# A two-layer fp32 encoder: mask by VectorE, an earlier-placed index selection, and an order of instructions from the tile framework's timeline simulator

## The chip, the cores and the metric

The kernel runs on one core of a Trainium2 chip. The metric is the device time of one execution in microseconds. The kernel before takes 315.13 us (median of three runs, 314.31 to 315.16).

## The reference

x has 256 tokens of 1024 features, fp32. Two layers follow one another, each with a gate and a post-norm. Layer 0 is attention over selected keys, layer 1 is stick-breaking attention, both with 16 heads of 64.

```python
# layer 0 (dsa_mixer): an indexer of 8 heads scores all keys, the best 64 admissible ones stay
q, k, v, g, qi, wi, ki = split(x @ w_in)          # q, k, qi, ki get rope
score = einsum('bqhs,bqh->bqs', relu(qi @ ki.T * 64 ** -0.5), wi)
idx = top_k(where(adm, score, -inf), 64)          # adm: key chunk <= query chunk, chunks of 64
o = softmax(where(selected, q @ k.T * 64 ** -0.5, -inf)) @ v
y = (o * silu(g)) @ w_out
# layer 1 (stick_breaking_mixer)
z = q @ k.T * 64 ** -0.5
log_one_minus = where(before, log_sigmoid(-z), 0)           # before: key position < query position
log_stick = cumsum(log_one_minus, reverse) - log_one_minus
y = ((where(before, exp(log_sigmoid(z) + log_stick), 0) @ v) * silu(g)) @ w_out
# after each layer
x = layer_norm(ALPHA * x + y, ln_g[i], ln_b[i])
```

## The kernel before

Every fp32 operand of a matmul is kept as a high part (rounded to the fp32r type by a ScalarE copy) and a low part (VectorE subtracts); `split` (L65) and `feat_split` (L247) do that, and a product is three matmuls: high by high, low by high, high by low. In the trace `wh`/`wl`, `xT`, `yT`, `zh`/`zl`, `oh`/`ol` are such pairs.

Weights come in 80 chunks of 128x1024 fp32 (512 KB) from `w_all`, by `fetch` (L79), through 4 raw buffers and 8 buffers each of `wh` and `wl`; a copy `wh` can start when its chunk has landed and the matmuls that read the buffer's former chunk are done. A chunk feeds 12 matmuls of 512 columns where an output block of 512 columns is computed for the two row blocks t = 0, 1 of 128 tokens (`tok_block`, L116), or one gate (`proj_feat`, L140: 24 matmuls of 256 columns).

Layer 0: the index projection runs over the 8 chunks of `x_idx` (L221 to L230), rope follows on VectorE (`rope`, L211), then `select` (L280) runs beside the q, k and v projections of the first half of the heads: score matmuls (L136 to L138 by `mm3`), Relu on ScalarE, weighting on VectorE, and eight rounds of max and match_replace per row block (L299, L300), which end in the masks `nm0` and `nm1` (L304). The head pairs pass through four stages in a loop of 11 steps (L525): `keys0`, `logits0` (min-reduce on VectorE L420, Exp on ScalarE L425, scaling of p by VectorE L430), `turn0` (transposes of p, L439 to L441, copy `pT` L443), `values0`. A generator `fill` puts the other projections, the eight gates and the out-projection between them. The out-projection with its norm is `out_norm` (L454): residual `z` (L461), statistics (L463, L467), power on GpSimd (L470), two passes over z and x (L473, L475); `turn` (L514) transposes x into `yT` for layer 1. The second row block's right half is computed in two banks of 256 columns.

Layer 1: v, the gates (`proj_feat1`, L148), then head pairs in five stages (L619); `logits1` (L564) adds the causal mask with an identity matmul (L576) and goes through Abs, Exp, Ln on ScalarE and a combination on VectorE (L582); `sticks1` sums along keys by matmuls with a triangle. Then `out_norm` again with stores.

Each engine works through its instructions in one fixed order. That order isn't the program's: the tile framework's scheduler sets it at build time from the dependences, except where `keep_in_program_order` pins an instruction. PSUM is shared by a pool `pp` of three banks and `at` of five.

## Time and profile before

| | |
|---|---|
| median of three runs | 315.13 us |
| profiled execution | 313.89 us, its span 312.1 us |
| TensorE busy | 299.8 us (96%), 1722 matmuls |
| VectorE busy | 246.3 us (79%) |
| ScalarE busy | 191.7 us (61%) |
| GpSimd busy | 7.7 us |
| DMA | 50.40 MB, mean 161 GB/s |

The span is that of one profiled execution; the run's time holds some 1.8 us around it. Busy shares are means over stages. The rows further down have times in us from the span's start.

### The profile page before, as it was taken

The numbers are of one execution on the slowest core, as the hardware profiler recorded it, in microseconds if no ns is written. First come the engines' busy times: TensorE is split into PE (matmuls) and PEld (weight loads), VectorE is DVE, ScalarE is ACT, GpSimd is POOL, SyncE is SP. The second block draws the span as 40 slices with busy tenths as digits, with TensorE's granted clock in tenths as the row PEclk, the third lists the DMA queues.
The fourth block names the chain that finished last, engine by engine and source line by source line (L and its number), as shares of the span: only waits on it lengthen the run. The fifth ranks groups of instructions, "written<-read, shape, count | busy, mean of one in ns | idle before, by whom it ended". The sixth has DMA issues, their size and how long they took to land.

```text
span 312.1 us, 4825 instructions
## 1 busy us (share of the span) xinstructions
PE 299.8 (96%) x1722; PEld 256.3 (82%) x1722; DVE 246.3 (79%) x538; ACT 191.7 (61%) x388; POOL 7.7 (2%) x16
## 2 busy tenths in 40 slices
PE   8998799998999999999999999999999999999990
PEld 5986688886888899988888888888888888887790
DVE  3777989998999999997589576776788887872375
ACT  5655445385346998875415377657799998975200
POOL 3010000000000000000010100000000000000011
PEclk9999799999999999999999999999999999999997
DMA  7898736586044846574424858866553253000003
GB/s 255 270 328 284 274 111 202 186 280 209 4 131 137 268 138 187 186 234 140 133 67 127 275 161 295 287 197 198 167 163 100 69 159 100 2 0 2 0 13 121
DMA packets 14423, 50.40 MB, mean 161 GB/s; under 512 B 1600, under 2 KB 1728, under 8 KB 14400
## 3 DMA queue, kind: packets, MB, share of 16 engines
q1 hardware_dynamic: 14256, 49.97, 49.3%
q8 instruction: 13, 0.21, 0.3%
q10 hardware_dynamic: 144, 0.14, 0.1%
q14 instruction: 10, 0.08, 0.1%
HBM read 49.05 MB, written 1.05 MB: 161 GB/s over the span
## 4 chain that ended last, share of the span: by engine, by line
PE 78%; DVE 10%; DMA 6%; issue 3%; ACT 2%; DVEq 0%; SPq 0%; ACTq 0%
PE bank L113 32%; PE bank L153 14%; PE bank L145 7%; PE bank L155 7%; DMA raw<-w_all 4%; DVE wl L67 4%; PE bank L368 3%; DMA raw<-x_idx 2%; PE bank L596 1%; PE bank L136 1%; PE bank L369 1%; DVE sc L293 1%; ACT wh L66 1%; DVE sc L300 1%; PE bank L138 1%
## 5 line engine op out<-in xcount | busy, mean ns | idle before, releaser
L67 DVE TENSOR_TENSOR wl<-raw,wh 128x1024 fp32r<-128x1024 f32 (+2 forms) x89 | 103.5, 1165 | 23.1 <-ACT wh L66 22.4
L66 ACT ACTIVATE wh<-raw 128x1024 fp32r<-128x1024 f32 (+2 forms) x89 | 90.0, 1016 | 50.2 <-DMA raw<-w_all 25.6
L113 PE MATMUL bank<-wh,xT 128*128 128x512 f32 x192 | 50.8, 400 | 1.2 <-DVE rb L216 1.2
L153 PE MATMUL bank<-yT,wh 128*128 128x512 f32 x192 | 48.3, 394 | 0.0
L113 PEld LDWEIGHTS bank<-wh,xT 128*128 128x128 f32 x192 | 35.9, 191 | 8.7 <-issue 1.6
L153 PEld LDWEIGHTS bank<-yT,wh 128*128 128x128 f32 x192 | 34.5, 189 | 6.9 <-issue 0.3
L155 PEld LDWEIGHTS bank<-yT,wl 128*128 128x128 f32 x192 | 26.2, 190 | 1.9
L113 PE MATMUL bank<-wl,xT 128*128 128x512 f32 x96 | 27.6, 396 | 0.0
L155 PE MATMUL bank<-yT,wl 128*128 128x256 f32 x192 | 26.8, 282 | 0.0
L113 PEld LDWEIGHTS bank<-wl,xT 128*128 128x128 f32 x96 | 18.4, 192 | 3.7
L113 PE MATMUL bank<-wh,ol 128*128 128x512 f32 (+1 forms) x80 | 20.5, 350 | 0.0
L113 PE MATMUL bank<-wh,oh 128*128 128x512 f32 (+1 forms) x80 | 20.4, 354 | 0.0
L113 PE MATMUL bank<-wl,oh 128*128 128x512 f32 (+1 forms) x80 | 20.2, 348 | 0.0
L113 PE MATMUL bank<-wh,yT 128*128 128x512 f32 x64 | 17.4, 391 | 0.0
L145 PE MATMUL bank<-xT,wh 128*128 128x256 f32 x128 | 16.9, 285 | 0.0
L425 ACT ACTIVATE p<-ml,mx 128x128 f32<-128x128 f32 (+1 forms) x32 | 14.3, 447 | 3.7 <-DVE mx L420 3.4
L145 PEld LDWEIGHTS bank<-xT,wh 128*128 128x128 f32 x128 | 16.1, 190 | 0.4
L113 PEld LDWEIGHTS bank<-wh,ol 128*128 128x128 f32 x80 | 14.1, 189 | 2.1 <-issue 0.2
L113 PEld LDWEIGHTS bank<-wl,oh 128*128 128x128 f32 x80 | 14.1, 189 | 1.9
L113 PEld LDWEIGHTS bank<-wh,oh 128*128 128x128 f32 x80 | 13.6, 189 | 2.2 <-issue 0.5
L113 PEld LDWEIGHTS bank<-wh,yT 128*128 128x128 f32 x64 | 12.0, 188 | 2.4
L582 DVE SCALAR_TENSOR_TENSOR ab<-bank,ab 128x512 f32<-128x512 f32 (+1 forms) x16 | 8.5, 555 | 6.3 <-ACT ab L581 5.9
(140 smaller groups left out, 507.3 us busy)
## 6 DMA issues: line engine op xcount, KB each, us to landing
raw<-w_all SPq DMA_DIRECT2D x80, 512.0 KB, 4.3
raw<-x_idx SPq DMA_DIRECT2D x7, 420.0 KB, 4.1
gb<-lnp SPq DMA_DIRECT2D x4, 512.0 KB, 6.9
x<-x_rows SPq DMA_DIRECT2D x2, 512.0 KB, 6.5
y<-x SPq DMA_DIRECT2D x4, 256.0 KB, 2.0
cs<-consts SPq DMA_DIRECT2D x1, 512.0 KB, 6.8
raw<-x_idx SPq DMA_DIRECT2D x1, 288.0 KB, 2.9
raw<-x_idx ACTq DMA_DIRECT2D x1, 132.0 KB, 3.1
```

What stands on the lines that cost most here:

```text
L66: nc.scalar.activation(h, src, AF.Copy)
L67: nc.vector.tensor_sub(lo, src, as32(h))
L113: nc.tensor.matmul(ps, src[kk][xp][:, t * P:(t + 1) * P], wc[wp][:, k, :], start=kk == 0 and xp + wp == 0, stop=kk == 7 and wp == 1)
L136: nc.tensor.matmul(ps, sh, mh, start=first, stop=False)
L138: nc.tensor.matmul(ps, sl, mh, start=False, stop=last)
L145: nc.tensor.matmul(ps, w[wp][:, k, :], src[k][xp], start=k + xp + wp == 0, stop=k == 7 and wp == 1)
L153: nc.tensor.matmul(ps, wh[:, k, :], yT[:, k], start=k == 0, stop=k == 7)
L155: nc.tensor.matmul(ps[:, :S], wl[:, k, :], yTh[:, k], start=False, stop=k == 7, skip_group_check=True)
L293: nc.vector.scalar_tensor_tensor(sc, rel[:, a, :], wi[t][:, h:h + 1], prev, op0=OP.mult, op1=OP.add)
L368: nc.tensor.matmul(po[rs, n * S:(n + 1) * S], vt[0][:, hs], p0(i), start=True, stop=False)
L425: nc.scalar.activation(p[:, i, :], m[:, i, :], AF.Exp, bias=mx[:, c], scale=-1.0, accum_out=sm[:, c])
L582: nc.vector.scalar_tensor_tensor(a, pv, 0.0, a, op0=OP.max, op1=OP.add)
```

## The change

What the source does differently, in the order of the program:

1. `load` pins the loads on SyncE's queue to the program's order. Before, layer 0's gains and biases (`gb`) and x's rows stood at places 17 to 23 of that queue, among the loads for the q and k blocks; now they stand at places 35 to 44, one after each step of the loop from step 4 on.
2. The first chunk of `x_idx` comes in three DMAs instead of two, chunks 1 and 3 are issued from ScalarE's queue, and VectorE copies the first `xT`.
3. `rope` adds both halves with one instruction, whose second operand has its halves swapped.
4. The transposes of the index queries and keys move into `select` and start two steps later; the scores of both row blocks are computed alternately, and both top-k follow.
5. p is scaled by ScalarE (a Copy with a scale per row) instead of VectorE.
6. The causal mask of layer 1 is added in PSUM by VectorE (16 adds of 128x256) instead of by 16 matmuls.
7. Layer 1's gains and biases are loaded inside its gate loop.
8. `schedule_with_timeline_sim=True`: the order of instructions on every engine comes from the framework's timeline simulator.

```diff
+    def load(dst, src):
+
+        tc.keep_in_program_order(nc.sync.dma_start(dst, src))
...
-        nc.sync.dma_start(raw, w_all[c])
+        load(raw, w_all[c])
...
         if k:
-            nc.sync.dma_start(raw, x_idx[k])
+            (nc.scalar.dma_start if k in (1, 3) else load)(raw, x_idx[k])
         else:
             first = S + IDX_A
-            nc.sync.dma_start(raw[:, :first], x_idx[k, :, :first])
-            nc.scalar.dma_start(raw[:, first:], x_idx[k, :, first:])
+            load(raw[:, :S], x_idx[k, :, :S])
+            nc.scalar.dma_start(raw[:, S:first], x_idx[k, :, S:first])
+            load(raw[:, first:], x_idx[k, :, first:])
...
+        if k:
+            split(xTh[:, k], xTl[:, k], raw[:, :S])
+        else:
+            nc.vector.tensor_copy(xTh[:, k], raw[:, :S])
+            nc.vector.tensor_sub(xTl[:, k], raw[:, :S], as32(xTh[:, k]))
...
-    cr = cst.tile([P, 3, P], F32R, name="cr")
-    nc.gpsimd.tensor_copy(cr, cs[:, :3 * P].rearrange("p (a b) -> p a b", a=3))
-    identr, trir, causr = cr[:, 0, :], cr[:, 1, :], cr[:, 2, :]
+    caus = cs[:, C_CAUS:C_CAUS + P]
+    trir = cst.tile([P, P], F32R, name="trir")
+    nc.gpsimd.tensor_copy(trir, cs[:, C_TRI:C_TRI + P])
...
-        nc.vector.tensor_add(dst[:, :, :32], a[:, :, :32], b[:, :, 32:])
-        nc.vector.tensor_add(dst[:, :, 32:], a[:, :, 32:], b[:, :, :32])
+        halves = [u.rearrange("p h (e d) -> p h e d", e=2) for u in (dst, a, b)]
+        nc.vector.tensor_add(halves[0], halves[1], halves[2][:, :, ::-1, :])
...
     def select():
-        for t in range(NT):
...
-            for j in range(4):
+        for _ in range(2):
+            yield
+        pt = bank(at)
+        for t in range(NT):
+            nc.tensor.transpose(pt[:, t * P:(t + 1) * P], ri[t][:, 8:10, :], ident)
+        pad_split(kz, pt[:, :S])
+        for j in range(2):
+            pt = bank(at)
...
+            feat_split(qih[:, 2 * j:2 * j + 2], qil[:, 2 * j:2 * j + 2], pv)
+        yield
+        scores = [sb.tile([P, (t + 1) * P], F32, name=f"sc{t}") for t in range(NT)]
+        for j in range(4):
             for t in range(NT):
...
+            yield
+        for t in range(NT):
+            sc = scores[t]
...
-                nc.vector.tensor_scalar(p[:, i, :], p[:, i, :], rc[:, c], None, op0=OP.mult)
+                nc.scalar.activation(p[:, i, :], p[:, i, :], AF.Copy, scale=rc[:, c])
...
+    def rows():
+        for t in range(NT):
+            load(x[t], x_rows[t * P:(t + 1) * P, :])
+            yield
+
+    extra = chain(rows(), load_gb(0))
     for s in range(NPAIR + 3):
-        if s == 4:
-            for t in range(NT):
-                nc.sync.dma_start(x[t], x_rows[t * P:(t + 1) * P, :])
-            load_gb(0)
+        if s >= 4:
+            next(extra, None)
...
-            nc.tensor.matmul(pv, kl[:, ks], z[0][:, :, qs], start=False, stop=False)
-            nc.tensor.matmul(pv[:, :, :P], identr, causr[:, None, :].to_broadcast([P, 2, P]),
-                             start=False, stop=True)
+            nc.tensor.matmul(pv, kl[:, ks], z[0][:, :, qs], start=False, stop=True)
+            nc.vector.tensor_add(pv[:, :, :P], pv[:, :, :P], caus[:, None, :].to_broadcast([P, 2, P]))
...
-    for _ in gates(ys):
-        pass
+    mix(gates(ys), chain((None for _ in range(2)), load_gb(1)))
...
-    with tile.TileContext(nc) as tc:
+    with tile.TileContext(nc, schedule_with_timeline_sim=True) as tc:
```

Point 8 moves instructions everywhere. Three places follow; line numbers of the changed kernel are 5 to 15 higher (L461 is L474 there, L518 is L532, L425 is L438, L430 is L443 and L443 is L456).

TensorE after the index projection, before. `ri0` and `ri1` are the index operands after rope, `bank_376` and `bank_377` the first q block.

```order
L113 MATMUL bank_376<-wl_289,xT_83 128x512 x2
L113 MATMUL bank_377<-wl_289,xT_83 128x512 x2
L264 MATMUL bank_330<-cs_168,ri0_298 128x128
L273 MATMUL bank_339<-cs_168,ri0_298 128x128
L273 MATMUL bank_346<-cs_168,ri0_298 128x128
L113 MATMUL bank_376<-wh_294,xT_83 128x512 x2
L113 MATMUL bank_377<-wh_294,xT_83 128x512 x2
L273 MATMUL bank_339<-cs_168,ri1_314 128x128
L273 MATMUL bank_339<-cs_168,ri0_298 128x128
L273 MATMUL bank_339<-cs_168,ri1_314 128x128
```

The same place of the changed kernel; 18 runs of two q matmuls stand between the index projection and the first row here, against 10 above.

```order
L118 MATMUL bank_352<-wh_368,xT_83 128x512 x2
L118 MATMUL bank_353<-wh_368,xT_83 128x512 x2
L118 MATMUL bank_352<-wh_368,xT_83 128x512 x2
L118 MATMUL bank_353<-wh_368,xT_83 128x512 x2
L284 MATMUL bank_408<-cs_169,ri0_299 128x128
L290 MATMUL bank_415<-cs_169,ri0_299 128x128
L290 MATMUL bank_422<-cs_169,ri0_299 128x128
L118 MATMUL bank_489<-wh_386,xT_83 128x512 x4
L118 MATMUL bank_352<-wl_369,xT_83 128x512 x2
L118 MATMUL bank_353<-wl_369,xT_83 128x512 x2
```

The first transposes of the index operands now come after 44 matmuls of the q block instead of 24, and the first score matmul after 108 matmuls of 512 columns instead of 43.

ScalarE around the first head pairs of layer 0, before. `p0_890` and `p1_903` are the first pair's probabilities for the two row blocks, `pT` their transposes' copies, `wh` weight copies.

```order
L249 ACTIVATE zh0_178<-bank_929 64x256
L425 ACTIVATE p0_890,sm_883<-ml0_889,mx_882 128x128 x2
L425 ACTIVATE p1_903,sm_883<-ml1_902,mx_882 128x256 x2
L249 ACTIVATE zh0_178<-bank_929 64x256
L66 ACTIVATE wh_1086<-raw_1084 128x1024
L66 ACTIVATE wh_1104<-raw_1102 128x1024
L443 ACTIVATE pT0_1057<-bank_1053 128x384
L425 ACTIVATE p0_1006,sm_999<-ml0_1005,mx_998 128x128
L252 ACTIVATE qh4_357<-bank_980 128x256
L425 ACTIVATE p0_1006,sm_999<-ml0_1005,mx_998 128x128
```

And now; the first pair is `p0_881` and `p1_894`, the second `p0_995` and `p1_1008`.

```order
L66 ACTIVATE wh_1629<-raw_1627 128x1024
L261 ACTIVATE zh1_183<-bank_1054 64x256
L66 ACTIVATE wh_1681<-raw_1679 128x1024
L66 ACTIVATE wh_1749<-raw_1747 128x1024
L438 ACTIVATE p1_894,sm_874<-ml1_893,mx_873 128x256 x2
L438 ACTIVATE p1_1008,sm_988<-ml1_1007,mx_987 128x256 x2
L443 ACTIVATE p1_894<-p1_894,rc_875 128x256 x2
L438 ACTIVATE p0_1105,sm_1098<-ml0_1104,mx_1097 128x128 x2
L456 ACTIVATE pT0_1046<-bank_1042 128x384
L443 ACTIVATE p1_1008<-p1_1008,rc_989 128x256 x2
L456 ACTIVATE pT1_1052<-bank_1048 128x384
```

Exps and scales of both pairs' p1 now follow the weight copies wh_1681 and wh_1749, whose buffers are those of gates 2 and 3 (`wh_1163` and `wh_1244`), and p0 of the first pair is long done.

VectorE at the end of layer 0's out-projection, before. `z_1684` and `x0_373` belong to the first row block, `z_1685` to the second, whose last two half banks are `bank_1938` and `bank_1965`.

```order
L461 SCALAR_TENSOR_TENSOR z_1684<-x0_373,bank_1887 128x512
L463 BN_STATS st_1686<-z_1684 128x6 x2
L467 BN_AGGR mv_1915<-st_1686 128x2
L469 TENSOR_SCALAR rs_1917<-mv_1915 128x1
L473 SCALAR_TENSOR_TENSOR z_1684<-z_1684,mv_1915,gb00_1165 128x512 x2
L475 SCALAR_TENSOR_TENSOR x0_373<-z_1684,rs_1917,gb01_1167 128x512 x2
L461 SCALAR_TENSOR_TENSOR z_1685<-x1_374,bank_1938 128x256
L67 TENSOR_TENSOR wl_2034<-raw_2031,wh_2033 128x1024
L67 TENSOR_TENSOR yT_375<-bank_1922,yT_375 128x4x128
L67 TENSOR_TENSOR yT_375<-bank_1931,yT_375 128x4x128
L463 BN_STATS st_1687<-z_1685 128x6
L461 SCALAR_TENSOR_TENSOR z_1685<-x1_374,bank_1965 128x256
```

And now; the first row block has `z_1673` and `x0_349`, the second `z_1674` with the half banks `bank_1927` and `bank_1954`.

```order
L67 TENSOR_TENSOR wl_2019<-raw_2016,wh_2018 128x1024
L480 BN_AGGR mv_1904<-st_1675 128x2
L67 TENSOR_TENSOR wl_2025<-raw_2022,wh_2024 128x1024
L474 SCALAR_TENSOR_TENSOR z_1674<-x1_350,bank_1954 128x256
L482 TENSOR_SCALAR rs_1906<-mv_1904 128x1
L486 SCALAR_TENSOR_TENSOR z_1673<-z_1673,mv_1904,gb00_1412 128x512 x2
L67 TENSOR_TENSOR wl_2057<-raw_2054,wh_2056 128x1024
L67 TENSOR_TENSOR wl_2063<-raw_2060,wh_2062 128x1024
L476 BN_STATS st_1676<-z_1674 128x6
L488 SCALAR_TENSOR_TENSOR x0_349<-z_1673,rs_1906,gb01_1553 128x512 x2
L480 BN_AGGR mv_1981<-st_1676 128x2
L482 TENSOR_SCALAR rs_1983<-mv_1981 128x1
```

The norm of x0, which ran ahead of both half-bank residuals, now runs behind them, with the weight splits wl_2025, wl_2057 and wl_2063 in between; these wait for copies whose buffers the matmuls of `bank_1954` release one after another.

TensorE at the same place, before.

```order
L113 MATMUL bank_1965<-wh_1808,ol2_1481 128x256
L518 MATMUL bank_1922<-cs_168,x0_373 128x128 x4
L113 MATMUL bank_1965<-wh_1808,ol3_1487 128x256
L113 MATMUL bank_1965<-wl_1809,oh2_1480 128x256
L518 MATMUL bank_1931<-cs_168,x0_373 128x128 x4
L113 MATMUL bank_1965<-wl_1809,oh3_1486 128x256
L113 MATMUL bank_1965<-wh_1865,oh4_1719 128x256
```

And now.

```order
L118 MATMUL bank_1954<-wl_1861,oh6_1824 128x256
L118 MATMUL bank_1954<-wl_1861,oh7_1830 128x256
L532 MATMUL bank_1911<-cs_169,x0_349 128x128 x4
L532 MATMUL bank_1920<-cs_169,x0_349 128x128 x4
L118 MATMUL bank_2028<-wh_1866,yT_351 128x512 x2
L118 MATMUL bank_2078<-wh_2018,yT_351 128x512 x2
L532 MATMUL bank_1988<-cs_169,x1_350 128x128 x4
L118 MATMUL bank_2028<-wh_1866,yT_351 128x512 x2
L118 MATMUL bank_2028<-wl_1867,yT_351 128x512 x2
```

x0's transposes (L518, now L532) stood among the matmuls of the last half bank and now stand behind its last one; x1's (bank_1988) come after four matmuls of layer 1 instead of 33.

## Rows read from the trace of the kernel before

**Rows 1.** The page, part 1: engine, busy us, share of the span, instructions.
```profile
PE 299.8 (96%) x1722; PEld 256.3 (82%) x1722; DVE 246.3 (79%) x538; ACT 191.7 (61%) x388; POOL 7.7 (2%) x16
```
**Rows 2.** All waits of TensorE: line, releaser, us in total, times, longest us.
```profile
PE bank L136 <- issue: 2.1, 1, 2.1
...
PE bank L113 <- DVE rb L216: 1.2, 1, 1.2
PE bank L264 <- DVE ri L238: 0.6, 1, 0.6
```
**Rows 3.** Timeline of ScalarE: start us, us, instruction, idle before it and its releaser.
```profile
29.75 1.06 ACT L66 ACTIVATE wh<-raw 128x1024 fp32r<-128x1024 f32 x1 [1.58 <-DMA raw<-w_all]
```
**Rows 4.** Stretches: us, busy (x instructions) of PE, PEld, DVE, ACT, POOL; clock, DMA, GB/s.
```profile
34.00:38.00 4.00, 4.00 (x15) 3.43 (x14) 3.97 (x9) 2.24 (x5) 0.00 (x0) 0.57 0.66 227
...
78.00:90.00 12.00, 12.00 (x55) 9.84 (x54) 11.94 (x39) 4.50 (x12) 0.00 (x0) 1.00 0.27 76
...
230.00:280.00 50.00, 49.99 (x308) 42.85 (x307) 40.94 (x77) 45.59 (x106) 0.00 (x0) 1.00 0.28 85
```
**Rows 5.** Timeline of TensorE at the seam between the layers.
```profile
163.62 0.63 PE L518 MATMUL bank<-cs,x 128*128 128x128 f32 x4
164.00 0.36 PE L113 MATMUL bank<-wh,ol 128*128 128x256 f32 x1
...
166.10 0.40 PE L113 MATMUL bank<-wl,oh 128*128 128x256 f32 x2
166.34 1.09 PE L113 MATMUL bank<-wh,yT 128*128 128x512 f32 x4
```
**Rows 6.** Timeline of ScalarE at the start: the first copy of xT.
```profile
3.70 0.42 ACT L66 ACTIVATE xT<-raw 128x256 fp32r<-128x256 f32 x1 [1.69 <-DMA raw<-x_idx]
```
**Rows 7.** Groups by line and shape, 205 to 300 us: busy us, mean ns, idle before.
```profile
L159 DVE TENSOR_TENSOR bank<-bank,low 128x256 f32<-128x256 f32 x20 | 8.5, 426 | 0.5 <-ACT low L158 0.4
...
L576 PE MATMUL bank<-cr 128*128 128x256 f32 x16 | 4.5, 279 | 0.0
```
**Rows 8.** Groups by line and shape, 60 to 165 us (same columns).
```profile
L66 ACT ACTIVATE wh<-raw 128x1024 fp32r<-128x1024 f32 x32 | 33.6, 1057 | 22.2 <-DMA raw<-w_all 11.5 <-PE bank L113 10.7
...
L425 ACT ACTIVATE p<-ml,mx 128x256 f32<-128x256 f32 x16 | 8.0, 501 | 1.4 <-DVE mx L420 1.2
...
L443 ACT ACTIVATE pT<-bank 128x384 f32<-128x384 f32 x16 | 7.0, 486 | 1.5 <-PE bank L441 1.5
...
L425 ACT ACTIVATION_READ_ACCUMULATOR p<-ml,mx 128x1 f32 x32 | 6.0, 189 | 0.0
...
L430 DVE TENSOR_SCALAR p<-p,rc 128x256 f32<-128x256 f32 x16 | 4.9, 349 | 0.1
...
L66 ACT ACTIVATE oh<-og 128x256 fp32r<-128x256 f32 x8 | 3.0, 412 | 3.2 <-DVE og L346 3.2
```
**Rows 9.** Timeline of VectorE at the seam.
```profile
161.08 0.26 DVE L467 BATCH_NORM_AGGREGATE mv<-st 128x2 f32<-128x24 f32 x1
...
161.45 1.41 DVE L473 SCALAR_TENSOR_TENSOR z<-z,mv,gb 128x512 f32<-128x512 f32 x2
162.78 1.41 DVE L475 SCALAR_TENSOR_TENSOR x<-z,rs,gb 128x512 f32<-128x512 f32 x2
164.10 0.41 DVE L461 SCALAR_TENSOR_TENSOR z<-x,bank 128x256 f32<-128x256 f32 x1
164.43 1.22 DVE L67 TENSOR_TENSOR wl<-raw,wh 128x1024 fp32r<-128x1024 f32 x1
165.57 1.47 DVE L67 TENSOR_TENSOR yT<-bank,yT 128x512 fp32r<-128x512 f32 x2
166.96 0.42 DVE L463 BATCH_NORM_STATS2 st<-z 128x6 f32<-128x256 f32 x1
```
**Rows 10.** Timeline of all engines in the tail: VectorE's norm and GpSimd's power.
```profile
306.26 1.41 DVE L473 SCALAR_TENSOR_TENSOR z<-z,mv,gb 128x512 f32<-128x512 f32 x2
306.48 0.92 POOL L470 TENSOR_TENSOR rs<-rs,mhalf 128x1 f32<-128x1 f32 x1 [4.24 <-DVE rs L469]
```

More of the change, by code (lines that the diff above doesn't have):

```diff
@@ L65, in split @@
     def split(h, lo, src):
-        nc.scalar.activation(h, src, AF.Copy)
+        copy = nc.scalar.activation(h, src, AF.Copy)
         nc.vector.tensor_sub(lo, src, as32(h))
+        return copy
     def feature_major(name):
@@ L188, in trunk @@
     cs = cst.tile([P, C_W], F32, name="cs")
-    nc.sync.dma_start(cs, consts)
+    load(cs, consts)
     ident = cs[:, C_ID:C_ID + P]
@@ L292, in select @@
                     h = 2 * j + a
-                    nc.vector.scalar_tensor_tensor(sc, rel[:, a, :], wi[t][:, h:h + 1], prev,
-                                                   op0=OP.mult, op1=OP.add)
-                    prev = sc
-                yield
+                    nc.vector.scalar_tensor_tensor(scores[t], rel[:, a, :], wi[t][:, h:h + 1],
+                                                   scores[t] if h else adm[t], op0=OP.mult, op1=OP.add)
+            yield
+        for t in range(NT):
+            sc = scores[t]
             for i in range(TOPK // 8):
@@ L524, in trunk @@
     fill = chain(k_block(1), q_block(1), v_block(1), gates(xs), out_norm(0, x, turn))
+    def rows():
+        for t in range(NT):
+            load(x[t], x_rows[t * P:(t + 1) * P, :])
+            yield
+    extra = chain(rows(), load_gb(0))
     for s in range(NPAIR + 3):
-        if s == 4:
-            for t in range(NT):
-                nc.sync.dma_start(x[t], x_rows[t * P:(t + 1) * P, :])
-            load_gb(0)
+        if s >= 4:
+            next(extra, None)
         for c in "kfvFlft":
```

33 lines of the change are left out of this document (12 added, 21 removed).

## The prediction

> **What bounds the kernel now.** I began with the busy times: TensorE is busy 96% of the span [rows 1], so the first question is where the other 4% sits. The list of TensorE's waits answers it: one hole of 2.1 us before the first score matmuls (L136), one of 1.2 us at L113, one of 0.6 us at L264 [rows 2]. The chain of instructions on ScalarE shows what made the largest: the weight copy at 29.75 had waited 1.58 us for its DMA, and the copies that the scores need stood behind it in ScalarE's queue [rows 3]. The reader should then look at the granted clock right after that hole: 0.57 in 34 to 38 us, against 1.00 in later stretches [rows 4]. So the hole is paid twice, once as idle time and once as 4.0 x 0.43 = 1.7 us of slow matmuls. From 78 us to the end of the matmuls TensorE hardly waits at all; in layer 1 (230 to 280 us) it is busy 49.99 of 50 us, with ScalarE at 45.59 close behind [rows 4]. Two places matter for what follows, because they are free of holes only through the order: the seam between the layers, where x0's transposes (163.62) stand among the last out-projection matmuls and the first matmul of layer 1 (166.34) follows without idle time [rows 5], and the tail. So the kernel is a full TensorE queue with some 5.6 us of curable loss. An order can gain those, and it can lose much more.
>
> **The change part by part.** All sums are made on the profiled run: a span of 312.1 us in a run of 313.89; the median of the three runs shown, 315.13, lies 1.2 above it.
>
> *Start.* The first xT copy leaves ScalarE, where it took 0.42 us ahead of the copy that TensorE waits for [rows 6]; the DMA of the first chunk is cut in three, and two later chunks go to ScalarE's queue, where they may land later. Between 0 and -0.8, taken: -0.4.
>
> *Index scores (18 to 38 us).* Before, 43 matmuls of 512 columns lie between the end of the index projection and the first score matmul; now 108 and 18 transposes do, as the order shows. At 12 matmuls per weight chunk that is 5 chunks more of cover for rope, splits and late DMAs, and x's rows and layer 0's gains and biases (2 MB) no longer stand among these loads. The two holes (0.6 + 2.1) [rows 2] and the slow clock (1.7) [rows 4] should go: -4.4. If the weights themselves arrive late, half stays: -2.2.
>
> *The hole at L113* (1.2 us, rope of the q block, VectorE) [rows 2]: the q block now comes later behind other work and rope has an add less per call. -1.2, or -0.6.
>
> *Causal mask.* 16 matmuls of 128x256 go [rows 7]; such matmuls start 0.12 us apart (two in the 0.24 us from 166.10 to 166.34) [rows 5], so 16 x 0.12 = 1.9 us of TensorE. 16 VectorE adds in PSUM come; the nearest row is the add of L159, 0.426 us [rows 7]: 6.8 us of VectorE, on the way from logits to Abs. TensorE is the bound there by a few per cent [rows 4], so most of the 1.9 is gained: -1.8; if ScalarE's 45.59 of 50 becomes the bound, 0.
>
> *Normalisation of p.* 32 VectorE operations (0.349 us for 128x256 [rows 8]) become ScalarE copies. The nearest row is ScalarE's copy of 128x256 from SBUF to SBUF, 0.412 us [rows 8]; with half of the 32 at 128x128 I estimate 0.38 for the mean, and 32 x 0.38 = 12 us more on ScalarE. The Trainium skill speaks against this ("ScalarE: Activation LUTs", Rules for kernel authors): multiplications belong on VectorE, and an activation costs about 0.3 us plus 0.83 ns per element; by that, an estimate from the page, a 128x256 copy is 0.51 us and the whole 15 us. The row is shorter than the page, and the sum goes by the row. What the move costs depends on where ScalarE stands in the way, which is the next term.
>
> *Top-k of the second half (D).* This is a move by the order. Before, the last index mask (nm1) was ready long before p1's transposes came up in TensorE's queue. Now VectorE computes it behind the weight split wl_1682, whose copy wh_1681 waits until gate 2's matmuls have let go of a weight buffer, and the exps of p1 stand on ScalarE behind wh_1749, which waits for gate 3's sixteen wh matmuls; call their end T3. From T3 TensorE has 8 more gate matmuls, 6 for logits and 2 transposes ahead of p1's transposes, some 2.2 us by the spacings above and 0.23 per 512 columns. ScalarE needs wh_1749 1.06, four exps with their accumulator reads (0.50 + 0.19, of which I estimate 0.1 to overlap: 2.3) and two scales (0.75, starts 0.38 apart) [rows 8], together 4.1 us: a hole of 1.9. Behind it the same queue holds two exps of p0, pT0_1046, two scales, pT1_1052, two exps, four scales and copies before pT0_1144; each of these is awaited by the next piece of TensorE's queue. Walked with 0.49 per pT, 0.50 to 0.58 per exp and 0.35 to 0.38 per scale [rows 8] the further holes are 0.7, 0.4 and 1.8. Sum +4.9, taken +5; if gates and fillers cover more than I see +2, with later holes of the same kind +8.
>
> *The seam (E).* Before, VectorE normalised x0 while TensorE ran the two half banks of the second row block; the whole norm took the stretch 161.08 to 164.1 [rows 9]. Now the order puts, on VectorE, the residual that reads the last half bank (bank_1954) ahead of x0's norm, and two weight splits inside it; and TensorE's queue has x0's transposes behind the last out-projection matmul. Let that matmul end at T. The copy wh_2018 waits for the buffer of wh_1779, which bank_1954's first matmuls release at T - 2.4; one copy per 1.06 us [rows 8] gives wh_2024 at T - 0.3, wh_2056 at T + 0.7, wh_2062 at T + 1.7. VectorE: wl_2025 to T + 1.2, residual 0.41 (1.6), rs 0.1 (aggregate and rs together 0.37, 161.08 to 161.45), two z of x0 1.41 (3.1), wl_2057 and wl_2063 at a start-to-start of 1.14 each (5.4), one bn_stats of 0.42 (5.8), two x0 1.41 (7.1; the first half at 6.5) [rows 9]. x0's transposes and copies allow four matmuls; then x1: aggregate and rs 0.4, z 1.41, x1 0.7 (9.6), and the low half of yT, 0.7 of 1.47 for two (10.3) [rows 9], which the next matmul reads. Up to T + 10.4 TensorE has 12 transposes (four from 163.62 to 164.00 [rows 5], so 1.2 us) and four matmuls of 0.23: 2.2 us. So the hole is 8.2 us where there was next to none [rows 5]. Bound below: without any wait on the copies the rows add up to 9.2, less 2.2 = 7.0. On top the clock: after a hole of 2.10 us it fell, and cost 1.7 [rows 2, 4]; after holes of 6 us and more I expect the same. +9.5; ends +7.0 and +10.5.
>
> *End of layer 1.* The order spends the two fillers from the out-projection earlier, so the last pairs' chains (logits, Abs, Exp, Ln, sticks, Exp) lie bare for a moment: +1, between 0 and +2.
>
> *Tail.* VectorE normalises x0 (z 1.41, x 1.41 [rows 9]) before the last residual of x1 and is still at it 1.1 us after the last matmul, where it waited for that matmul before: +1.1, ends 0.5 and 1.5.
>
> Hidden at no cost: the smaller cast of trir, the loads of layer 1's gains inside the gate loop, which nothing reads before the tail, and the rope adds elsewhere. If the loads did delay a weight chunk, that would be another hole of about 1 us, which the range holds.
>
> Sum: -0.4 - 4.4 - 1.2 - 1.8 + 5 + 9.5 + 1 + 1.1 = +8.8. The profiled run would take 322.7, the median of runs about 324.0.
>
> **The rivals.** *Covered (faster or the same).* ScalarE has slack elsewhere in layer 0 (it is busy 4.50 of 12 us before 90 us [rows 4]); if its queue runs ahead, so that p1 is ready when its transposes come, D and the end of layer 1 cost nothing and only the seam and the tail are paid. Price: -8.2 (start at its best) + 7.0 + 0.5 = -0.7, with the seam at its lower bound and no clock loss: 313.2 for the profiled run, 314.4 for the median; -7.8 + 7.0 + 1.1 = +0.3 gives 315.4, and a seam that overlaps some 2 us more than I see 312.5. Against it: wh_1749 can't start before T3, whatever ScalarE did earlier, because the buffer isn't free. It decides when the hole before p1's transposes is under 0.5 us.
>
> *Clock (slower still).* Each of the holes near 2 us in D could drop the clock as the one at 30.75 did [rows 2, 4], while after the hole at L113, of 1.2 us, 78 to 90 us is at 1.00 [rows 2, 4]. Twice 1.7 more and D at its upper end: 324 + 3.4 + 3 = 330.
>
> *VectorE and GpSimd block each other.* In the seam GpSimd's power (0.92 us) comes between rs and x. The trace shows VectorE's z of 306.26 running 1.41 us, its usual time, with the power from 306.48 beside it [rows 10]. If they excluded each other, each norm in the seam would be 0.9 longer: 324 + 1.8 = 325.8. The Trainium skill has that rule ("SBUF — State Buffer", Summary: rules for kernel authors): with two SBUF inputs on VectorE and GpSimd reading SBUF, the second to issue blocks fully. The row disagrees for this pair.
>
> **How the numbers follow.** Forecast 0.60: 324.0, with its own range 318 to 329. Covered 0.22: 0.14 of it under 314.2, 0.08 within 0.3% of 315.13, 314.2 to 316.1 (about what a measurement of this kernel tells from no change). Clock 0.15. Blocking 0.03. So faster 0.14, same 0.08, slower 0.78. The range leaves out a tenth at each side: 313.5 to 331.
>
> **What would show it.** In the changed trace: no hole and clock 1.00 at 18 to 40 us; TensorE's waits with a group at the p1 transposes (L453 of the changed kernel) of about 2 us and smaller ones behind it; in the seam x0's transposes (L532 there) waiting some 6.5 us for VectorE's x0, two wl splits between z and x0, and a clock under 1.00 after it; layer 1 with about 0.1 us less per logits block. I am wrong if x0's transposes wait less than 4 us, or if p1's don't wait; if both, the time is about 310 and the order has done what it is there for.

## Result, and the profile after

The changed kernel takes 333.8 us (median of four runs, 332.51 to 337.45) against 315.14 for the kernel before, a ratio of 1.061 with a 95% interval of 1.052 to 1.070. The direction was forecast, the size was not: +18.7 us instead of +8.8, above the upper end of the range (313.5 to 331). The profiled execution took 332.51, its span 330.7 us. Each ratio compares with executions of the kernel before that were taken in the same session (their medians are 312.7 to 313.5 us with the experiments), so experiments are set against the changed kernel by their ratios. One of e7's four executions lies over 1.5% above its fastest and is left out of e7's figures.

The page's busy times (answering [rows 1]): TensorE has 16 matmuls fewer, yet it is busy longer, for a smaller share of a longer span.

```profile
PE 306.3 (93%) x1706; PEld 255.2 (77%) x1706; DVE 242.7 (73%) x511; ACT 204.3 (62%) x419; POOL 7.3 (2%) x16
```

TensorE's waits (answering [rows 2]; line, releaser, us in total, times, longest):

```profile
PE bank L532 <- issue: 6.3, 1, 6.3
PE bank L590 <- ACT kh L261: 2.0, 2, 1.0
PE bank L452 <- ACT p L443: 1.3, 1, 1.3
PE bank L381 <- ACT pT L456: 1.2, 2, 0.6
PE bank L172 <- DVE rest L169: 1.2, 1, 1.2
PE bank L118 <- ACT oh L66: 1.0, 1, 1.0
PE bank L150 <- DVE sg L406: 0.8, 1, 0.8
PE bank L381 <- ACT aw L618: 0.8, 1, 0.8
PE bank L141 <- DVE mx L433: 0.8, 2, 0.5
```

The reader should see that none of the three holes named in [rows 2] is left. L136, L113 and L264 are L141, L118 and L284 here: L284 has no line, L141 now waits for VectorE's mx of the logits and L118 for layer 1's oh. L172 belongs to the matmuls at the very start and is in both kernels (L167 before, 1.2 us too). New holes have come: L532 is the seam (x0's transposes), L452, L381 with pT, L150 and L141 lie in 107 to 127 us, the stretch called D, and L590, L381 with aw and L118 lie in layer 1.

Stretches of the changed kernel (answering [rows 4]; us, busy time and instructions of PE, PEld, DVE, ACT, POOL, granted clock, DMA share, GB/s):

```profile
34.00:38.00 4.00, 4.00 (x20) 3.24 (x19) 4.00 (x7) 3.13 (x5) 0.00 (x0) 1.00 0.64 234
...
230.00:280.00 50.00, 47.26 (x270) 39.26 (x270) 38.81 (x73) 41.42 (x90) 0.00 (x0) 1.00 0.40 127
170.00:180.00 10.00, 3.72 (x15) 3.01 (x14) 9.96 (x19) 3.00 (x4) 1.91 (x2) 0.70 0.69 210
180.00:190.00 10.00, 10.00 (x47) 8.27 (x46) 2.70 (x5) 1.79 (x3) 0.00 (x0) 0.95 0.01 2
110.00:120.00 10.00, 8.80 (x53) 6.21 (x53) 4.55 (x27) 9.90 (x35) 0.00 (x0) 1.00 0.18 55
```

34 to 38 us is at full clock now (0.57 before). The loss has moved to the seam, where TensorE has 3.72 us of work in ten, and into layer 1, where it is busy 47.26 us of 50 instead of 49.99.

**Where the time went.** A list of waits shows only holes. To see everything, I gave each matmul the start-to-start time that it has undisturbed (16 matmuls of 256 columns from 119.39 to 121.29 us: 0.119 each; 0.227 for 512 columns; 0.109 for transposes of 128; 0.110 and 0.060 for value matmuls of 256 and 128 columns that stand in pairs), added these in each kernel's own order, and took the sum off the real start. What is left is the time lost up to that moment in the profiled execution, idle or slow, in us:

| up to, us | before | after | source alone | order alone |
|---|---|---|---|---|
| 20 | 6.2 | 6.1 | 6.2 | 8.6 |
| 80 | 12.6 | 6.9 | 11.2 | 9.4 |
| 130 | 13.5 | 15.3 | 12.2 | 17.2 |
| 170 | 14.8 | 19.4 | 14.9 | 21.1 |
| 190 | 14.8 | 28.2 | 14.9 | 30.5 |
| 280 | 17.2 | 35.0 | 17.2 | 33.9 |
| end | 19.0 | 39.0 | 19.3 | 38.3 |

"Source alone" and "order alone" are the first two experiments. The changed kernel is 5.7 us ahead at 80 us, has given that back by 130, and then loses 9 us at the seam, where the kernel before loses nothing, and 11 in layer 1, where that loses 4. Its 16 missing matmuls take 1.9 us off the sum of undisturbed times, and the tail adds 0.5 behind the last matmul.

### The profile page after: what moved, and what is told of

The parts are those of the page before. It is cut to its first block, busy times and chain, and to the rows that moved or that the text cites. A ratio compares the mean times of both kernels' runs of the same rounds, so it can differ in the third digit from the quotient of the medians.

```text
span 330.7 us, 4843 instructions
## 1 busy us (share of the span) xinstructions
PE 306.3 (93%) x1706; PEld 255.2 (77%) x1706; DVE 242.7 (73%) x511; ACT 204.3 (62%) x419; POOL 7.3 (2%) x16
## 4 chain that ended last, share of the span: by engine, by line
PE 85%; ACT 6%; DVE 5%; issue 3%; DVEq 0%
PE bank L118 40%; PE bank L158 12%; PE bank L150 7%; PE bank L160 5%; PE bank L240 4%; PE bank L381 3%; ACT wh L66 2%; DVE wl L67 1%; PE bank L382 1%; PE bank L141 1%; PE bank L143 1%; PE bank L142 1%; PE bank L172 1%; PE bank L612 1%; PE bank L532 1%
## 5 line engine op out<-in xcount | busy, mean ns | idle before, releaser
L118 PE MATMUL bank<-wh,xT 128*128 128x512 f32 x192 | 51.8, 393 | 0.0
L158 PE MATMUL bank<-yT,wh 128*128 128x512 f32 x192 | 48.8, 393 | 0.7 <-DVE zl L265 0.4
L118 PEld LDWEIGHTS bank<-wh,xT 128*128 128x128 f32 x192 | 35.5, 188 | 7.0
L158 PEld LDWEIGHTS bank<-yT,wh 128*128 128x128 f32 x192 | 34.6, 188 | 7.6 <-issue 0.8
L118 PE MATMUL bank<-wl,xT 128*128 128x512 f32 x96 | 28.3, 391 | 0.0
L118 PE MATMUL bank<-wh,oh 128*128 128x512 f32 (+1 forms) x80 | 21.2, 357 | 1.1 <-ACT oh L66 1.0
L118 PE MATMUL bank<-wh,ol 128*128 128x512 f32 (+1 forms) x80 | 21.5, 354 | 0.0
L118 PE MATMUL bank<-wl,oh 128*128 128x512 f32 (+1 forms) x80 | 20.7, 349 | 0.0
L118 PEld LDWEIGHTS bank<-wl,xT 128*128 128x128 f32 x96 | 17.9, 188 | 3.7
L118 PE MATMUL bank<-wh,yT 128*128 128x512 f32 x64 | 18.6, 410 | 0.0
L150 PE MATMUL bank<-xT,wh 128*128 128x256 f32 x128 | 17.2, 286 | 0.8 <-DVE sg L406 0.8
L150 PEld LDWEIGHTS bank<-xT,wh 128*128 128x128 f32 x128 | 16.2, 191 | 1.5 <-DVE sg L406 1.3
L118 PEld LDWEIGHTS bank<-wh,oh 128*128 128x128 f32 x80 | 13.8, 189 | 3.8 <-ACT oh L66 2.0
L118 PEld LDWEIGHTS bank<-wh,ol 128*128 128x128 f32 x80 | 13.8, 189 | 2.5 <-issue 0.9
L118 PEld LDWEIGHTS bank<-wl,oh 128*128 128x128 f32 x80 | 13.9, 189 | 2.0 <-issue 0.2
L438 ACT ACTIVATE p<-ml,mx 128x128 f32<-128x128 f32 (+1 forms) x32 | 14.2, 449 | 1.3 <-DVE mx L433 1.3
L118 PEld LDWEIGHTS bank<-wh,yT 128*128 128x128 f32 x64 | 12.3, 197 | 2.6 <-ACT yT L66 0.2
L443 ACT ACTIVATE p<-p,rc 128x128 f32<-128x128 f32 (+1 forms) x32 | 12.6, 448 | 0.4 <-DVE rc L440 0.4
```

The source lines that it names most:

```text
L118: nc.tensor.matmul(ps, src[kk][xp][:, t * P:(t + 1) * P], wc[wp][:, k, :], start=kk == 0 and xp + wp == 0, stop=kk == 7 and wp == 1)
L150: nc.tensor.matmul(ps, w[wp][:, k, :], src[k][xp], start=k + xp + wp == 0, stop=k == 7 and wp == 1)
L158: nc.tensor.matmul(ps, wh[:, k, :], yT[:, k], start=k == 0, stop=k == 7)
L438: nc.scalar.activation(p[:, i, :], m[:, i, :], AF.Exp, bias=mx[:, c], scale=-1.0, accum_out=sm[:, c])
L443: nc.scalar.activation(p[:, i, :], p[:, i, :], AF.Copy, scale=rc[:, c])
```

## Experiments

My theory: the fixed order is the loss, through instructions placed behind others that wait; the edits of the source are worth a little. The rivals: an edit of the source (p on ScalarE, the later scores, the mask) is the loss; or VectorE's load, or its sharing with GpSimd.

### The two halves of the change

`e1_source_alone` has all edits of the source and the usual scheduler; `e2_order_alone` is the source of before with the simulator's order.

```diff
-    with tile.TileContext(nc, schedule_with_timeline_sim=True) as tc:
+    with tile.TileContext(nc) as tc:
```

> All edits of the source, but the order from the framework's usual scheduler as before. Theory (the order costs the time): the lost time of the seam between the layers (8.8 us) and most of that at 80 to 130 us (7.5 us) go, no wait of 6 us at x0's transposes; 306 to 314 us. Rival (the source's edits cost it: late index selection, p scaled on ScalarE, mask added on VectorE): the waits at p's transposes and in layer 1 stay, 318 to 326 us.

> The source of before with the timeline simulator's order as the only change. Theory (the order costs the time): slower than before by 10 to 20 us, with a hole of 5 us or more at x0's transposes in the seam: 325 to 336 us. Rival (the source's edits cost it): only the seam's hole shows, within 9 us of before: 315 to 324 us.

Source alone: 310.42 us, ratio 0.993 (0.990 to 0.996). Order alone: 334.99 us, 1.069 (1.065 to 1.073). The order is the whole loss, and the source alone beats both kernels, by 0.7% the one before. The waits of the order alone are much like those of the changed kernel (the seam, mx, oh and kh), though its source has p on VectorE, early scores and the mask as matmuls (lines are those of before, [rows 2]):

```profile
PE bank L518 <- issue: 6.3, 1, 6.3
PE bank L228 <- ACT wh L66: 2.5, 1, 2.5
PE bank L136 <- DVE mx L420: 2.2, 1, 2.2
PE bank L113 <- ACT oh L66: 1.9, 2, 1.0
...
PE bank L573 <- ACT kh L249: 1.0, 1, 1.0
```

With the source alone, TensorE has no hole from 80 to 130 us while ScalarE is as full as in the changed kernel (9.93 us of 10 from 110 to 120 here, 9.90 there). So ScalarE's load alone does not make the holes; what stands in its queue does.

```profile
110.00:120.00 10.00, 10.00 (x84) 9.87 (x83) 8.85 (x25) 9.93 (x33) 0.00 (x0) 1.00 0.57 187
```

### The seam repaired

`e3_seam_pinned` holds the weight splits of layer 1 and the residuals of the last half bank behind x0's norm, and puts the out-projection's last matmuls behind x0's transposes. `e5_seam_with_splits` does the same and holds the splits behind the low half of x0's yT instead of behind the norm. In the diff, of e3, `done[0]` is x0's last norm instruction and `turned` has x0's last transpose of each half.

```diff
-                    tok_part([(t, ps)], og, [w[:, :, cols[0]:cols[1]] for w in ws[c]], c)
-                residual(t, 512 + cols[0], ps)
+                    late = layer == 0 and cols[0] == 256 and c >= 2
+                    with tc.issue_after(turned[0, c - 2].ins) if late else nullcontext():
+                        tok_part([(t, ps)], og, [w[:, :, cols[0]:cols[1]] for w in ws[c]], c)
+                with tc.issue_after(done[0].ins) if layer == 0 and t else nullcontext():
+                    residual(t, 512 + cols[0], ps)
...
-                wv[n] = list(load_block())
+                with tc.issue_after(done[0].ins):
+                    wv[n] = list(load_block())
```

> The changed kernel, with x0's norm pinned on VectorE ahead of both residuals of the second row block's right half, x0's transposes pinned on TensorE among the matmuls of the last half bank, and the splits of layer 1's first weights behind the norm. Theory (the seam's order costs 8.8 us by itself): 333.8 - 8.5 = 325 us, the wait of 6.3 us at x0's transposes gone and the clock at 1.00 there. Rival (the time is only moved, the first matmuls of layer 1 wait for something else): 330 to 334 us.

> As the pinned seam, and the splits of layer 1's first weights stand behind the low half of yT as well. Theory (the hole of 3.0 us that stayed was four weight splits ahead of yT's low half): the lost time between the last out-projection and layer 1 goes from 4.6 to about 1.5 us, 328 to 329.5 us. Rival (the time moves on to the weights that are split later): 331 to 333 us.

e3: 331.52 us, 1.057 (1.052 to 1.063). Against the changed kernel's 1.061 (1.052 to 1.070) that is a gain of 0.3%, not clear of the noise. The hole did not close, it moved: the simulator now puts four splits between x0's norm and the low half of yT that the next matmul reads. VectorE and then TensorE of e3:

```profile
171.55 4.63 DVE L67 TENSOR_TENSOR wl<-raw,wh 128x1024 fp32r<-128x1024 f32 x4
...
176.43 1.27 DVE L67 TENSOR_TENSOR yT<-bank,yT 128x512 fp32r<-128x512 f32 x2
```

```profile
173.08 1.09 PE L118 MATMUL bank<-wh,yT 128*128 128x512 f32 x4
177.16 0.73 PE L118 MATMUL bank<-wh,yT 128*128 128x512 f32 x2 [2.98 <-DVE yT L67]
```

e5: 327.57 us, 1.049 (1.043 to 1.055), 1.2% or some 3.8 us less than the changed kernel, though the two intervals overlap a little. By the sum above its seam loses 2.7 us instead of 8.8, 6.1 less; not all of that reached the end. In the execution with the profile, which took 330.31, a wait of 2.4 us at L158 for VectorE's sg appears at 213 us, where the changed kernel has 0.3 (at 216.72); VectorE has an add to a bank (L164) ahead of that sg there, which stands behind it in the changed kernel. Both runs say that the seam's loss is its order, on VectorE and of x0's transposes; and that one repaired place lets the simulator order the next ones anew, so that no edit under the simulator's order changes one thing alone.

### p, the mask, the scores and GpSimd

`e4_p_on_vector` is the changed kernel with p scaled by VectorE again.

```diff
-                nc.scalar.activation(p[:, i, :], p[:, i, :], AF.Copy, scale=rc[:, c])
+                nc.vector.tensor_scalar(p[:, i, :], p[:, i, :], rc[:, c], None, op0=OP.mult)
```

> The changed kernel with p scaled by VectorE again, the timeline simulator's order kept. Theory (ScalarE as the bound at 105 to 130 us costs about 4 us, the late index mask the rest): 329 to 331 us, ScalarE no longer busy 9.9 of 10 us there. Rival (the scaling on ScalarE is the whole loss at 80 to 130 us): 326 us. Second rival (VectorE is as short there): 333 to 335 us.

336.9 us, 1.074 (1.068 to 1.081): no gain, if anything 1.3% worse, with 2.2 us of waiting for mx before the logits, as in the order alone. So the move of p alone does not make D's holes.

`e7_index_mask_early` is the changed kernel with the splits of the gates' weights held behind the last index mask, `nm1`.

```diff
-        split(wh, wl, raw)
+        with tc.issue_after(picked[0].ins) if 24 <= c < 44 else nullcontext():
+            split(wh, wl, raw)
...
-            nc.vector.tensor_scalar(nm, sc, 0.9 * NEG_REP, -NEG_BIG, op0=OP.is_gt, op1=OP.mult)
+            picked[:] = [nc.vector.tensor_scalar(nm, sc, 0.9 * NEG_REP, -NEG_BIG, op0=OP.is_gt, op1=OP.mult)]
```

> The changed kernel, with the splits of the gates' weights pinned on VectorE behind the last index mask (nm1), so that the top-k of the second row block is done before them. Theory (the late mask opens the holes at 105 to 130 us): the lost time there goes from 8.4 to about 3 us, 327 to 330 us, no wait at p's transposes. Rival (VectorE, busy 10.0 of 10 us at 90 to 100, is short and the gates now wait for their weights): 333 to 336 us.

336.45 us, 1.078 (1.071 to 1.086). The mask comes at 91.9 us instead of 106.3, and p's transposes wait 0.4 us instead of 1.3, but the gates now wait 2.9 us for th. The stretch 100 to 130 us loses 10.1 us by the sum, not less than before the repair.

`e8_selection_later` and `e13_scores_late` are the source alone with the scores 4 and 8 steps late instead of 2.

```diff
-        for _ in range(2):
+        for _ in range(8):
             yield
```

> The source's edits under the usual order, with the index selection started four steps later instead of two. Theory (in the source alone the index transposes still come too early for rope and the weight copies, 2 to 3 us of holes up to 80 us): 308 to 309.5 us. Rival (the later top-k then holds up the first head pairs): 311 to 314 us.

> The source's edits under the usual order, with the index selection started eight steps later instead of two: 120 matmuls of 512 columns before the first score matmul (43 before, 108 in the changed kernel). Theory (late scores alone cost the stretch at 100 to 130 us: the gain at the start is given back by the mask): lost time there 5 to 8 us, ratio to before 1.010 to 1.022. Rival (the usual order takes late scores without a hole, so that the simulator's placing of the steps behind them is the cause): 0.990 to 1.001.

e8: 312.43 us, 0.998 (0.995 to 1.002). e13: 310.73 us, 0.992 (0.989 to 0.996), as fast as the source alone, with its last mask at 92.2 us, 0.3 from where e7 has it. Under the usual order late scores, and a mask at 92.2 instead of 82.9 us, cost nothing that can be told from the source alone; a mask as late as the changed kernel's 106.3 was not tried there.

`e9_mask_by_matmul` and `e12_source_mask_by_matmul` put the causal mask back to matmuls, in the changed kernel and in the source alone.

```diff
-            nc.tensor.matmul(pv, kl[:, ks], z[0][:, :, qs], start=False, stop=True)
-            nc.vector.tensor_add(pv[:, :, :P], pv[:, :, :P], caus[:, None, :].to_broadcast([P, 2, P]))
+            nc.tensor.matmul(pv, kl[:, ks], z[0][:, :, qs], start=False, stop=False)
+            nc.tensor.matmul(pv[:, :, :P], identr, causr[:, None, :].to_broadcast([P, 2, P]),
+                             start=False, stop=True)
```

> The changed kernel with the causal mask added by the 16 matmuls again, the simulator's order kept. Theory (under this order the VectorE adds lie bare between logits and Abs, which with ScalarE near its limit makes the new holes at 230 to 260 us): lost time in layer 1 falls by 3 us against 1.9 us more of matmuls, ratio to before 1.050 to 1.058. Rival (the holes there come from the order of the kh copies on ScalarE whatever adds the mask): 1.063 to 1.069.

> The source's edits under the usual order, but with the causal mask by matmuls as before. Theory (the mask's move is worth its 1.9 us of matmuls there, since layer 1 waits for TensorE alone): ratio 0.997 to 1.001 where the source alone had 0.9927. Rival (VectorE's adds eat it): 0.991 to 0.995.

e9: 333.56 us, 1.064 (1.056 to 1.071), no difference from the changed kernel. e12: 312.42 us, 0.998 (0.995 to 1.002) against 0.993 without: the mask's move is worth 0.56% or 1.8 us (0.3 to 3.2) where TensorE has no holes.

`e10_splits_on_gpsimd` and `e11_source_and_gpsimd` let GpSimd compute seven of the low halves between chunks 10 and 32, in the changed kernel and in the source alone.

```diff
-        split(wh, wl, raw)
+        if 10 <= c < 32 and c % 3 == 0:
+            nc.scalar.activation(wh, raw, AF.Copy)
+            nc.gpsimd.tensor_sub(wl, raw, as32(wh))
+        else:
+            split(wh, wl, raw)
```

> The changed kernel with 7 of the 22 weight splits of chunks 10 to 31 on GpSimd instead of VectorE, some 8 us of VectorE's work in the stretch from 40 to 110 us. Theory (VectorE, busy over 9 of 10 us there, is the second bound, so that what TensorE gains before 40 us is given back at 105 to 130 us): lost time at 100 to 130 us falls from 8.4 to 4 us or less, ratio 1.040 to 1.050. Rival (the order is to blame there, not the load): 1.056 to 1.066; if GpSimd and VectorE hold each other up, 1.07 and more.

> The source's edits under the usual order, with the same 7 splits on GpSimd. Theory (VectorE is the second bound up to 130 us): the holes up to 80 us (some 3 us) go, ratio 0.983 to 0.990. Rival (TensorE's queue is what counts, VectorE's relief hides): 0.991 to 0.996. If a split on GpSimd takes longer than the chunk's lead, slower than before.

e10: 332.89 us, 1.063 (1.055 to 1.070): taking seven splits off VectorE leaves the time where it was. That does not clear VectorE's load: by the sum, 100 to 130 us loses 4.8 us instead of 8.4, near what the theory asked for, and 20 to 100 us loses 4.7 instead of 0.8. Nor is the load as much lighter as meant: VectorE is busy 3.1 us less from 40 to 110 us, where some 8 were moved. What speaks against the load is that the source alone has VectorE busy 66.2 of the 72 us from 38 to 110 us (the changed kernel 70.5) and no hole in D behind it, and that VectorE is busy only 4.55 of ten where the changed kernel's holes lie, from 110 to 120 us. e11: 314.86 us, 1.006 (1.003 to 1.009), 1.3% over the source alone. Groups by line and shape from 38 to 110 us (busy us, mean ns, idle before), e11 first:

```profile
L67 DVE TENSOR_TENSOR wl<-raw,wh 128x1024 fp32r<-128x1024 f32 x18 | 25.3, 1407 | 1.1 <-ACT wh L66 1.1
...
L95 POOL TENSOR_TENSOR wl<-raw,wh 128x1024 fp32r<-128x1024 f32 x7 | 16.8, 2399 | 68.6 <-ACT wh L94 68.6
...
L234 DVE TENSOR_TENSOR kr<-ra,rb 128x512 f32<-128x512 f32 x4 | 4.3, 1063 | 0.0
```

```profile
L67 DVE TENSOR_TENSOR wl<-raw,wh 128x1024 fp32r<-128x1024 f32 x23 | 27.8, 1213 | 1.2 <-ACT wh L66 1.1
...
L230 DVE TENSOR_TENSOR kr<-ra,rb 128x512 f32<-128x512 f32 x4 | 2.7, 676 | 0.0
```

The second fence is the source alone. Beside GpSimd's splits of 2.4 us VectorE's own take 1407 ns in the mean instead of 1213 and the rope's add 1063 instead of 676, and TensorE's wait for rope is 3.8 us instead of 0.9. The means hide that single operations are held: of the four adds one takes 2.22 us, the one that starts beside a split of GpSimd, and it ends 0.55 us behind that split; the other three take their usual 0.68. The two rows of e11's timeline:

```profile
48.97 2.41 POOL L95 TENSOR_TENSOR wl<-raw,wh 128x1024 fp32r<-128x1024 f32 x1 [29.06 <-ACT wh L94]
...
49.71 2.22 DVE L234 TENSOR_TENSOR kr<-ra,rb 128x512 f32<-128x512 f32 x1
```

### The value matmuls

The sum of lost time showed something that no wait shows. The two heads of a pair write the two partition halves of one bank (`po[rs]`), in matmuls of 64 columns of weights; the trace shows each of them as two, and counts below are the trace's. Before, the matmuls of both heads stand together; a piece of TensorE's timeline of before, then one of the changed kernel:

```profile
106.23 0.66 PE L368 MATMUL bank<-pT,vt 128*64 128x256 f32 x4
106.72 0.39 PE L369 MATMUL bank<-pT,vt 128*64 128x128 f32 x4
106.94 0.65 PE L368 MATMUL bank<-pT,vt 128*64 128x256 f32 x4
```

```profile
111.55 0.65 PE L381 MATMUL bank<-pT,vt 128*64 128x256 f32 x2 [0.62 <-ACT pT L456]
...
112.35 0.33 PE L453 MATMUL bank<-cs,p 128*128 128x128 f32 x1
...
112.93 0.65 PE L381 MATMUL bank<-pT,vt 128*64 128x256 f32 x2
```

Before, eight matmuls take 0.71 us to the next start (106.23 to 106.94): the two heads' run side by side. In the changed kernel one head's four take 0.80 (111.55 to 112.35), and the other head's come after transposes. The start-to-start time of layer 0's 64 value matmuls, waits left out, is 6.06 us before and 9.44 after; of layer 1's 6.69 and 7.41.

`e6_values_as_block` makes the four value matmuls of two heads one critical block in the changed kernel; `e14_values_by_half` goes the other way, in the source alone: all matmuls of the one half, then all of the other.

```diff
+            with tc.tile_critical():
                 for i in range(2):
```

```diff
-        for n, (j, p0, p1) in enumerate(weights):
-            for i in range(2):
+        for i in range(2):
+            for n, (j, p0, p1) in enumerate(weights):
...
+                with tc.issue_after(prev.ins) if prev else nullcontext():
```

> The changed kernel, with the four value matmuls of a head pair (both heads, both key blocks) issued as one block. Theory (the heads' value matmuls write to different halves of the partitions and run side by side only when they stand together): their time in layer 0 goes from 9.4 back to 6.1 us; up to 4 us less in all, 330 to 332 us, if the block's wait for both copies of p costs nothing. Rival (what is gained is waited for, since the second head's copy comes late): the slots shrink but the waits grow by as much, 333 to 335 us.

> The source's edits under the usual order, but each group of value matmuls goes first through the first heads of both pairs (one half of the partitions), then through the second heads, instead of alternating. Theory (two of them run side by side only when neighbours in the queue write to different halves): 16 groups lose most of the overlap, value matmuls 13.6 to 20 to 25 us, ratio 1.010 to 1.035. Rival (the engine finds the other half's matmuls further down its queue): value matmuls within 2 us of 13.6, ratio 0.990 to 1.000.

e6: 353.86 us, 1.129 (1.123 to 1.136). The matmuls stand in pairs again, but a block waits for all its inputs and everything behind it waits too, some 14 us in waits at the block's first line alone. Layer 0's value matmuls still take 9.45 us, not the 6.1 expected: the clock is low behind several of these waits, and some 0.1 to 0.25 us of idle time follows most blocks. It says nothing of what pairs are worth.

e14: 314.77 us, 1.003 (1.000 to 1.005) against 0.993: splitting the heads costs 1.0% (0.6 to 1.4), 3 us, between what the theory and the rival expected. Its value matmuls take 8.71 and 8.85 us in the two layers instead of 6.55 and 7.04, 4.0 more; its waits are 1.8 us shorter than the source alone's. The timeline shows the pairing directly:

```profile
104.22 0.65 PE L383 MATMUL bank<-pT,vt 128*64 128x256 f32 x2
...
104.92 0.65 PE L383 MATMUL bank<-pT,vt 128*64 128x256 f32 x4
...
105.63 0.59 PE L383 MATMUL bank<-pT,vt 128*64 128x256 f32 x2
```

Four matmuls of one head alone take 0.70 us (104.22 to 104.92), and eight, where the last of the one half meets the first of the other, take 0.71 (104.92 to 105.63).

## Why the prediction was right or wrong

| term | forecast | measured | judgement |
|---|---|---|---|
| start | -0.4 | 0 (6.2 and 6.1 lost up to 20 us) | no gain |
| index scores and hole at L113 | -5.6 | -5.6 (20 to 80 us) | right |
| causal mask | -1.8 | -1.9 in undisturbed times; 0 (e9) and -1.8 (e12) in the time | right, but hidden under this order |
| D, 80 to 130 us | +5 | +7.5, of it 4.1 in waits | waits right, the rest unforeseen |
| 130 to 170 us | none | +2.8 | unforeseen |
| seam | +9.5 | +8.8 | right, its clock loss counted on top of the hole |
| layer 1 to 280 us | none | +4.4, of it 3.0 in waits | unforeseen |
| end of layer 1 | +1 | +2.2 | just above its end of +2 |
| tail | +1.1 | +0.5 | at its lower end |

**Right: the index scores.** No hole, and 34 to 38 us at clock 1.00. This gain is mostly the order's: from 20 to 80 us the kernel before loses 6.4 us, the source alone 5.0 (its waits at L284, L240 and L141 remain), the order alone and the changed kernel 0.8.

**Right: the seam.** The prediction had x0's transposes at T + 7.1 at the latest, T being the end of the last out-projection matmul, and two splits between z and x. VectorE there (answering [rows 9]):

```profile
170.31 1.16 DVE L67 TENSOR_TENSOR wl<-raw,wh 128x1024 fp32r<-128x1024 f32 x1
...
171.78 1.40 DVE L486 SCALAR_TENSOR_TENSOR z<-z,mv,gb 128x512 f32<-128x512 f32 x2
173.10 2.35 DVE L67 TENSOR_TENSOR wl<-raw,wh 128x1024 fp32r<-128x1024 f32 x2
...
175.71 1.40 DVE L488 SCALAR_TENSOR_TENSOR x<-z,rs,gb 128x512 f32<-128x512 f32 x2
```

And TensorE (answering [rows 5]):

```profile
169.87 0.40 PE L118 MATMUL bank<-wl,oh 128*128 128x256 f32 x2
176.55 1.94 PE L532 MATMUL bank<-cs,x 128*128 128x128 f32 x8 [6.28 <-issue]
178.32 2.07 PE L118 MATMUL bank<-wh,yT 128*128 128x512 f32 x4
180.19 0.95 PE L532 MATMUL bank<-cs,x 128*128 128x128 f32 x4
180.90 0.71 PE L118 MATMUL bank<-wh,yT 128*128 128x512 f32 x2
...
181.91 1.07 PE L118 MATMUL bank<-wh,yT 128*128 128x512 f32 x4
```

The page names no releaser for the 6.28 us, but VectorE's rows do: it is busy without a break from 170.31 until x's two halves, and the transposes start 0.84 us after the first of these starts. The clock fell as forecast: four matmuls take 2.07 us at 178.32 and 1.07 at 181.91. The idle time is 6.3 us instead of 8.2, and the slow matmuls behind it cost 2.3 by the sum instead of 1.3. The two errors belong together: T is 170.27, and the matmul behind x1's transposes starts at 180.90, T + 10.6 where the forecast had T + 10.4, so the slow matmuls filled time that the forecast had as idle, and its clock loss should not have come on top of the hole.

**Right in mechanism, short in size: D.** ScalarE's rows show the step of the prediction: a weight copy that waits for the gate's matmuls, four exps behind it, then the scales, and p's transposes waiting 1.3 us for them.

```profile
105.85 1.06 ACT L66 ACTIVATE wh<-raw 128x1024 fp32r<-128x1024 f32 x1 [1.82 <-PE bank L150]
107.06 0.51 ACT L438 ACTIVATE p<-ml,mx 128x256 f32<-128x256 f32 x1 [0.16 <-DVE mx L433]
...
109.31 0.91 ACT L443 ACTIVATE p<-p,rc 128x256 f32<-128x256 f32 x2 [0.17 <-DVE rc L440]
```

The forecast walked 1.9 + 0.7 + 0.4 + 1.8 us of holes (4.8, where it has 4.9); the waits from 80 to 130 us are 1.3 + 1.2 + 0.8 + 0.8 = 4.1. A scale took 0.501 us for 128x256 and 0.395 for 128x128 (L443), 0.45 in the mean against 0.38 forecast; the copy that the price was taken from has no scale per row. Since neighbours overlap, the 32 add 12.6 us of busy time, close to the forecast's 12.

What failed here is that "the change part by part" let D cost only its waits. It took the matmuls' own times as given, whatever stands beside them. Value matmuls that lost their neighbours cost 1.8 us up to 130 us, 1.6 from there to 170 and 0.7 in layer 1, together 4.1 by the sum of start-to-start times; e14 shows that such a loss reaches the end (3 us for 4.0). The other 1.6 of D lies mostly in transposes and logits that stand alone between other matmuls.

**Wrong: the stretches without a term.** This is the step that failed. The prediction took the seam and the tail as the places that are free of holes only through the order, walked these, D and the end, and let the rest stand. The sum fell short by 9.9 us: 7.2 of them lie in stretches that have no term (2.8 from 130 to 170 us, 4.4 from 190 to 280), 2.5 in D, 1.2 in the end of layer 1 and 0.4 in the start, while seam, tail and mask came out 1.4 below their terms. From 190 to 280 us 3.0 of the 4.4 are waits. There the order has ScalarE's kh, which the logits read, behind a weight copy that waits for its buffer; ScalarE's rows, then the wait on TensorE:

```profile
232.82 1.06 ACT L66 ACTIVATE wh<-raw 128x1024 fp32r<-128x1024 f32 x1 [1.08 <-PE bank L158]
...
234.31 0.38 ACT L261 ACTIVATE kh<-bank 128x256 fp32r<-128x256 f32 x1
```

```profile
234.75 0.62 PE L590 MATMUL bank<-zh,kh 128*128 128x512 f32 x2 [1.01 <-ACT kh L261]
```

It is D's mechanism again, and could have been walked in the order as D was. The second wait of L590, 1.0 us at 251.19, is of another kind: kh starts at 250.75, behind work of ScalarE without a break, of which the copy at 248.04 waits for no buffer. The end is as forecast in kind (aw 0.8 and oh 1.0, with no filler left), 1.2 us over its term.

**The rivals.** Covered is refuted: D's holes are there. Clock is refuted for the changed kernel, where 110 to 120 us is at 1.00, but not as a mechanism: with the order alone the hole of 2.25 us at 111.93 is followed by the stretch below, at 0.57.

```profile
112.00:116.00 4.00, 4.00 (x14) 2.40 (x15) 3.53 (x21) 3.98 (x17) 0.00 (x0) 0.57 0.41 123
```

Blocking by GpSimd's power has no row in its favour: z at 171.78 takes 1.40 us as before. But z starts ahead of the power in both traces (power at 172.01 here), so these rows test that rival only weakly.

**What stays open.** Which placement first sets D back is not settled. The early mask (e7), p on VectorE (e4), fewer splits on VectorE (e10) each left the loss or moved it, each with a new order throughout, and late scores cost nothing under the usual order (e13). What is shown is that the order alone brings it (7.8 us lost from 80 to 130 us in e2, 1.0 in e1). Nor was the out-projection's part of 130 to 170 us traced to a cause; its matmuls lose 1.1 us more there than before.
